# One decoder step on one core: the first attention operands loaded during the decode, and the fourth w_up split moved from GpSimd to VectorE

## The chip, the cores and the metric

The kernel runs on one core of a Trainium2 chip. The metric is the time of one execution on the device in microseconds (us). The core has five engines that work side by side, each through its own queue of instructions in order: TensorE (PE, matrix products; PEld is its loading of weights), VectorE (DVE), ScalarE (ACT), GpSimd (POOL) and SyncE (SP, which here only issues DMAs). GpSimd issues DMAs too. An instruction that waits for a semaphore holds up everything behind it on its engine.

## The reference: what is computed

One layer of a decoder over two inputs: a prompt of 1024 tokens and 8 samples of 4 new tokens each with 1024 cached positions. Model width is 1024.

```python
h = rms_norm(x, n1) * (1 + sc1) + sh1
q_a, k_a, v_a, q_b, f_b, i_b, g_b = split(h @ w_in)
q_a, k_a = rms_norm(q_a, qg), rms_norm(k_a, kg)
o_a = stick_breaking(q_a, k_all, v_all, positions, sb_b)      # 8 heads of 64
o_b = hgrn2(...)                                              # gated recurrence, 8 heads of 64
x = x + g1 * (concat(o_a, o_b) @ w_out)
h2 = rms_norm(x, n2) * (1 + sc2) + sh2
x = x + g2 * (square(relu(h2 @ w_up)) @ w_down)               # w_up 1024 x 4096
```

For the prompt, keys and values are those of the prompt itself. For the samples, `k_all` and `v_all` are read from a paged cache through a page table (64 pages of K, 64 of V, 128 positions each) with the new tokens behind them; that part is called the decode here. In stick-breaking attention the weight of a key is sigmoid(z) times the product of 1 - sigmoid(z') over the keys between it and the query, which the kernel takes with a reversed cumulative product (a scan) over each row.

## The kernel before, in words

Products are made in float32r with both operands split into a high and a low part: hi is a cast of x (ScalarE, line 151), lo is x - hi (line 152). Each product is then three matmuls: hi by hi, lo by hi, hi by lo. A piece of a weight is 128 x 1024: `weight` (line 154) loads it into wraw (2 buffers), casts it into whi and subtracts into wlo (5 buffers each), at a raised priority. The argument `e` names the engine of the subtraction, VectorE where nothing is given.

The work goes in stages: projections, recurrence with the attention of the first 512 prompt tokens, output projection of those tokens, then from about 550 to 1100 us the stage of this change, then the output projection of the other 512 and the sample tokens, and their MLP up to the end. q and k of the prompt are written to DRAM (`qkd`, high and low parts) early on, and read back head by head.

In the stage of the change two chains of work are interleaved on the engines (line 1470). One is the first MLP (`mlp`, line 1183), which runs 8 blocks of 512 columns of w_up; in a block four pieces of w_up (m = 0 to 3), then four pieces of w_down. `GL = (3,)` gives the subtraction of the fourth piece to GpSimd. The other chain is `decode_and_attention` (line 1439): first the decode of the samples (`decode`, line 563), its later part beside the recurrence of the samples (`hgrn_decode`, line 962), then the attention of the second 512 prompt tokens (`attention`, line 879) over 8 heads.

For each head the attention loads qh and ql (line 891, both halves of the partitions hold the same 64 rows) and kk (line 892, high and low part of k) and vhl (line 894). All are issued by GpSimd, two buffers each, from a pool that is opened once the decode's pools are closed. Then for each 128 queries: z = two products (lines 905, 906), sigmoids on ScalarE (909, 910), masks on GpSimd (913, 914), the scan on VectorE (919), a product on GpSimd (920), transposes on PE (932), the split into wh and wl (151, 152), and the products with V (941, 942).

The recurrence of the samples loads its states s0b (line 972) by GpSimd as well, two for each step and half, each once the half before is used.

The order of instructions on an engine is not written out by hand. The tile framework plans it before the run, from the order of emission, raised priorities and a timeline of its own (`schedule_with_timeline_sim=True`, line 1507).

The first MLP's pool (`rp`, line 1465) holds one g2b tile of 128 x 1024 and two xres tiles of 128 x 512. In before these are written in the last block of the MLP only.

Of the kernel before, what the change touches and what calls it, by code (L numbers as in the profile page):

```python
# [9 lines left out]
F32 = mybir.dt.float32  # L10
F32R = mybir.dt.float32r
# [9 lines left out]
P = 128  # L21
D = 1024
KT = 8
T = 1024
# [9 lines left out]
NBE0, NBE, NHB, NWA, NU, NRW, NX2, NF = 4,8,3,4,4,4,3,3  # L34
ORDER = (4,5,8,6,7)
NWH, NOM, SPL, NRAW, NRC, NAT = 2,3,7,4,2,1
PV, PQ, PW, PH = [162, 417, 315, 427]
GL, GD = (3,),()
BO = dict(o="0167", r="45")
KS0 = "wwwwwuup"  # L40
KS1 = "5p 0w 6p 1w 7p 2w 3u 4u"
# [40 lines left out]
def hymba_step(ctx, tc, x_p, x_s, ck, cv, st_in, ptab, c_p, c_s, w_ada, b_ada, n1g, n2g, w_in,  # L82
# [3 lines left out]
    V, S, G, TE = nc.vector, nc.scalar, nc.gpsimd, nc.tensor  # L86
# [14 lines left out]
    def pool(name, side="left", stack=ctx, **kw):  # L101
        return stack.enter_context(tc.tile_pool(name=name, bufs=1, side=side, reuse_waits="tile", **kw))
# [7 lines left out]
    qkd = dp.tile([2, 2, 4, P, T], F32, name="qkd")  # L110
# [449 lines left out]
                                nc.sync.dma_start(qkd[what, part, 2 * p2:2 * p2 + 2, :, rows].rearrange("a p t -> p a t"),  # L560
                                                  tt.rearrange("p a u t -> p a (u t)").bitcast(F32))

    def decode(pd_):

        qbd = pd_.tile([P, 2, 544], F32, name="qbd", tag="qbd", bufs=1)
        G.memset(qbd, 0.0)
# [38 lines left out]
        ms = pd_.tile([P, 4, NB, 4], F32, name="ms")  # L605
# [35 lines left out]
        for gz in range(2):  # L641
            be = bes[gz]

            qbf = pd_.tile([P, 4, 32], F32, name="qbf")
            G.memset(qbf, 0.0)
            for p in range(4):
                for hh in range(2):
                    rr, o = slice(64 * hh, 64 * hh + 64), 4 * hh
# [15 lines left out]
            for k0 in (0, 4, 8):  # L664
                n, r = (4, P) if k0 < 8 else (1, NS)
# [9 lines left out]
            for b4 in range(4):  # L675
                b = 4 * gz + b4
# [18 lines left out]
                for hh in range(2):  # L695
                    r = slice(64 * hh, 64 * hh + 64)
# [179 lines left out]
        with tc.high_priority(offset=PH):  # L876
            norm()

    def attention(pb, ms, nbe):

        q0, nq, nk = 256 * ms[0], 256 * len(ms), 256 * (ms[-1] + 1)
        both = lambda t, part, p, r, cs: qkd[t, part, p, r, cs].unsqueeze(0).to_broadcast([2, 64, cs.stop - cs.start])
        for p in range(4):
            for hh in range(2):
                h = 2 * p + hh
                hr = slice(64 * hh, 64 * hh + 64)

                qh, ql = (pb.tile([P, nq], F32R, name=name, bufs=2) for name in ("qh", "ql"))
                kk_ = pb.tile([P, nk], F32R, name="kk", bufs=2)
                for part, tile_ in enumerate((qh, ql)):  # L890
                    G.dma_start(tile_, both(0, part, p, hr, slice(q0, q0 + nq)))
                G.dma_start(kk_, qkd[1, :, p, hr, 0:nk])
                vhl = pb.tile([P, nk // P, P], F32R, name="vhl", bufs=2)
                G.dma_start(vhl, vd[0:nk, P * h:P * (h + 1)].rearrange("(t p) x -> p t x", p=P))
                for m in ms:
                    ws = []
                    for i in (2 * m, 2 * m + 1):
                        n = (i + 1) * P
# [26 lines left out]
                    for kb in range(0, 2 * m + 2, 2):  # L925
# [12 lines left out]
                        for a in range(2):  # L938
                            cs = slice(P, 256) if diag and a == 1 else slice(0, 256)
# [22 lines left out]
    def hgrn_decode(p1):  # L962
# [63 lines left out]
        for j in range(4):  # L1026
# [10 lines left out]
             lambda n, p=ga: p.tile([P, 2048], F32, name="wada", bufs=NAR)[:, 0:512 * n], "ada")  # L1037
# [4 lines left out]
    qstack.close()  # L1042
    gh = hgrn(pool("hgrn", stack=gstack))
    gb = attention(pool("attn0", stack=astack), (0, 1), NBE0)

    def until(g, x):
# [136 lines left out]
    def mlp(h_hi, h_lo, chunks, fp, nx, side=iter(())):  # L1183
# [1 line left out]
        r_hi = [h_hi[:, k] for k in range(KT)]  # L1185
        r_lo = [h_lo[:, k] for k in range(KT)]
        n = chunks[-1].stop
        g2b = fp.tile([P, D], F32, name="g2b")
        acc = [lp.tile([P, HW], F32, name=f"acc{c}", tag="acc", bufs=8) for c in range(KT)]
        for blk in range(NBLK):  # L1190
            u_hi, u_lo, ws = [], [], []
# [20 lines left out]
            if blk == 0:  # L1212
                for cs in parts:
                    for m in range(NK):
                        up(m, cs)
                    yield
            if blk == NBLK - 1:
                nc.sync.dma_start(g2b, g2d.to_broadcast([P, D]))
            for half_ in range(2):

# [218 lines left out]
    def decode_and_attention():  # L1439
        banks.update(BD)  # L1440
        with ExitStack() as es:
            gd = decode(pool("decode", stack=es))
            for _ in range(33):
                next(gd)
                yield
            banks.update(BV)
            yield from side_by_side((gd, 28), (hgrn_decode(pool("hgrn_s", stack=es)), W[4]))
        banks.update(BA)
        with ExitStack() as es:
            yield from attention(pool("attn1", stack=es), (2, 3), NBE)  # L1450

    def h2_tiles():
        return hp2.tile([P, KT, HW], F32R, name="h2_hi", tag="h2_hi", bufs=1), hp2.tile([P, KT, HW], F32R, name="h2_lo", tag="h2_lo", bufs=1)
# [11 lines left out]
    rp = pool("res", side="right", stack=rstack)  # L1465
# [45 lines left out]
```

## Time and profile before

| | us |
|---|---|
| median of 3 runs | 1550.24 |
| lowest, highest run | 1548.09, 1552.9 |
| profiled execution | 1546.85 |
| its span, first to last instruction | 1545.1 |
| TensorE busy in the span | 1489.3 (96%) |
| VectorE busy | 1083.4 (70%) |
| ScalarE busy | 642.7 (42%) |
| GpSimd busy | 345.4 (22%) |

All views below are of the profiled execution, with times in us from the start of its span. A busy time is the sum over an engine's instructions; "idle before" with an arrow says how long the engine stood still before an instruction and what ended the wait. The granted clock is a share of TensorE's full clock of 2.4 GHz.

### The profile page before, as it was taken

The page shows a single profiled execution, that of the slowest core. Times are in us where ns is not written, and L with a number is a line of the kernel's source. Part 1 is how long each engine was busy: PE and PEld are TensorE (multiplying, and loading weights), DVE is VectorE, ACT ScalarE, POOL GpSimd, SP SyncE. Part 2 cuts the span into 40 slices and gives each one's busy share as a digit, 9 for nine tenths or more (in the row PEclk, how much of TensorE's full clock was granted, in tenths as well). Part 3 has the DMA queues.
Part 4 walks back from the last instruction along what each step waited for, and adds up shares of the span by engine and source line. Part 5 has one row for each costly group of instructions (what it writes and reads, how often), then busy time and mean ns, then how long its engine had stood idle before and what let it go on. Part 6 is the DMA issues. An engine that isn't in the chain of part 4 may idle for free. (4 is left out here: it accounts for less than half of the span.)

```text
span 1545.1 us, 26232 instructions
## 1 busy us (share of the span) xinstructions
PE 1489.3 (96%) x9521; PEld 1257.0 (81%) x9521; DVE 1083.4 (70%) x2288; ACT 642.7 (42%) x1219; POOL 345.4 (22%) x560
## 2 busy tenths in 40 slices
PE   7999999999999989999997999999999999999998
PEld 3666689999999787775665788888578999999998
DVE  4976438888876783455554888888688567777775
ACT  3742234443422454333232666664245533343340
POOL 0200125634210030000121676694200000000000
PEclk8999999999999999999998999999999999999999
DMA  9389873423123456668677366552654333323222
GB/s 325 118 278 309 265 231 68 106 58 92 37 77 114 140 172 219 218 216 256 199 160 121 88 133 121 119 113 74 237 164 125 105 96 96 92 84 99 84 82 86
DMA packets 249414, 223.14 MB, mean 144 GB/s; under 512 B 60507, under 2 KB 196259, under 8 KB 247236
## 3 DMA queue, kind: packets, MB, share of 16 engines
q1 hardware_dynamic: 186308, 199.26, 41.0%
q0 software_dynamic: 62976, 22.20, 8.8%
q8 instruction: 75, 1.23, 0.3%
q14 instruction: 55, 0.45, 0.1%
HBM read 190.14 MB, written 31.11 MB: 143 GB/s over the span
## 5 line engine op out<-in xcount | busy, mean ns | idle before, releaser
L204 PE MATMUL pm<-h_hi,whi 128*128 128x384 f32 (+3 forms) x800 | 273.0, 343 | 6.0 <-DVE h_hi L335 3.0
L205 PE MATMUL pm<-h_lo,whi 128*128 128x384 f32 (+3 forms) x800 | 272.2, 341 | 0.3
L206 PE MATMUL pm<-h_hi,wlo 128*128 128x384 f32 (+3 forms) x800 | 271.7, 340 | 0.0
L151 ACT CAST whi<-wraw 128x1024 fp32r<-128x1024 f32 x136 | 142.8, 1053 | 217.8 <-PE pm L205 128.0
L152 DVE TENSOR_TENSOR wlo<-wraw,whi 128x1024 fp32r<-128x1024 f32 x128 | 169.1, 1321 | 89.6 <-ACT whi L151 83.6
L204 PEld LDWEIGHTS pm<-h_hi,whi 128*128 128x128 f32 x800 | 151.5, 190 | 24.3 <-issue 6.4
L206 PEld LDWEIGHTS pm<-h_hi,wlo 128*128 128x128 f32 x800 | 152.1, 190 | 10.6 <-issue 2.0
L205 PEld LDWEIGHTS pm<-h_lo,whi 128*128 128x128 f32 x800 | 152.2, 190 | 10.2 <-DVE h_lo L336 0.8
L206 PE MATMUL pm<-uh,wlo 128*128 128x272 f32 x512 | 145.2, 289 | 0.0
L205 PE MATMUL pm<-ul,whi 128*128 128x272 f32 x512 | 144.8, 288 | 0.0
L204 PE MATMUL pm<-uh,whi 128*128 128x272 f32 x512 | 139.8, 289 | 0.4 <-ACT uh L1327 0.4
L919 DVE TENSOR_TENSOR_SCAN om<-om 128x128 f32<-128x128 f32 (+3 forms) x96 | 112.3, 1174 | 25.4 <-POOL om L913 20.3
L1228 PE MATMUL pm<-whi,uh 128*128 128x512 f32 x256 | 104.7, 409 | 3.3 <-DVE acc L1236 3.3
L920 POOL TENSOR_TENSOR be<-be,om 128x384 f32<-128x384 f32 (+3 forms) x96 | 100.5, 1056 | 23.9 <-DVE om L919 20.0
L1229 PE MATMUL pm<-wlo,uh 128*128 128x512 f32 x256 | 101.9, 399 | 0.0
L1230 PE MATMUL pm<-whi,ul 128*128 128x512 f32 x256 | 101.7, 402 | 0.0
L205 PEld LDWEIGHTS pm<-ul,whi 128*128 128x128 f32 x512 | 95.9, 188 | 0.2 <-DVE ul L1328 0.2
L206 PEld LDWEIGHTS pm<-uh,wlo 128*128 128x128 f32 x512 | 95.9, 188 | 0.1
L204 PEld LDWEIGHTS pm<-uh,whi 128*128 128x128 f32 x512 | 93.4, 188 | 0.7 <-ACT uh L1327 0.7
L217 PE MATMUL pm_qkv<-whi,h_lo 128*128 128x512 f32 x192 | 77.3, 403 | 1.1 <-DVE h_lo L336 0.8
L215 PE MATMUL pm_qkv<-whi,h_hi 128*128 128x512 f32 x192 | 77.2, 403 | 0.4 <-DVE rs_i L138 0.3
L216 PE MATMUL pm_qkv<-wlo,h_hi 128*128 128x512 f32 x192 | 76.4, 398 | 0.0
(404 smaller groups left out, 3408.5 us busy)
## 6 DMA issues: line engine op xcount, KB each, us to landing
wraw<-in_w_down_dram SPq DMA_DIRECT2D x64, 512.0 KB, 5.7
wraw<-in_w_up_dram SPq DMA_DIRECT2D x40, 512.0 KB, 5.6
wada<-in_w_ada_dram SPq DMA_DIRECT2D x16, 1024.0 KB, 8.7
raw<-in_cache_k_dram SPq DMA_DIRECT2D x64, 256.0 KB, 3.2
vt<-in_cache_v_dram SPq DMA_DIRECT2D x64, 256.0 KB, 4.6
wraw<-in_w_in_dram SPq DMA_DIRECT2D x24, 512.0 KB, 5.9
uraw<-in_w_up_dram SPq DMA_DIRECT2D x24, 512.0 KB, 3.8
wa<-in_w_ada_dram SPq DMA_DIRECT2D x16, 512.0 KB, 6.4
```

The costliest lines, as they stand in the source:

```text
L151: (V.tensor_copy if h is V else S.copy)(hi, src)
L152: (e or V).tensor_tensor(lo, src, hi.bitcast(F32), op=sub)
L204: TE.matmul(pm, w_hi[:, k, :], r_hi[k][:, cs], start=(k == ks[0]), stop=False)
L205: TE.matmul(pm, w_hi[:, k, :], r_lo[k][:, cs], start=False, stop=False)
L206: TE.matmul(pm, w_lo[:, k, :], r_hi[k][:, cs], start=False, stop=(k == ks[-1]))
L215: TE.matmul(pm, h_hi[:, k, cs], hi, start=(k == 0), stop=False)
L217: TE.matmul(pm, h_lo[:, k, cs], hi, start=False, stop=(k == KT - 1))
L919: V.tensor_tensor_scan(back, back, back, 1.0 if right is None else right[:, 0:1], op0=mult, op1=ALU.bypass)
L920: G.tensor_tensor(be[:, 0:w], be[:, 0:w], om[:, 1:w + 1], op=mult)
L1228: TE.matmul(pm, u_hi[m][:, ts], hi, start=(m == 0), stop=False)
L1229: TE.matmul(pm, u_hi[m][:, ts], lo, start=False, stop=False)
L1230: TE.matmul(pm, u_lo[m][:, ts], hi, start=False, stop=(m == NK - 1))
```

## The change

Four edits in one:

1. `GL` is empty, so the fourth piece of w_up in each block of the first MLP is split on VectorE, as the other three are.
2. The three loads qh, ql and kk are made a function `load_qk`. For head 0 of the second attention it is called inside `decode`, behind the memset of qbf of the second group of samples, and told to be issued after that memset.
3. The tiles of these three loads are taken from the first MLP's pool: qh0 and ql0 in the two buffers of xres, kk0 in the buffer of g2b. The first attention is as before.
4. The tile g2b of the first MLP is taken in the last block, in the same buffer.

vhl of head 0, and all loads of the other heads, stay where they are.

```diff
-GL, GD = (3,),()
+GL, GD = (),()
...
-    def decode(pd_):
+    def decode(pd_, first):
...
-            G.memset(qbf, 0.0)
+            mark = G.memset(qbf, 0.0)
+            if gz == 1:
+                with tc.issue_after(mark.ins):
+                    load_qk(*first, 0, 512, 512, T)
...
+    def load_qk(qh, ql, kk, h, q0, nq, nk):
+
+        hr = slice(64 * (h % 2), 64 * (h % 2) + 64)
+        for part, x in enumerate((qh, ql)):
+            G.dma_start(x, qkd[0, part, h // 2, hr, q0:q0 + nq].unsqueeze(0).to_broadcast([2, 64, nq]))
+        G.dma_start(kk, qkd[1, :, h // 2, hr, 0:nk])
...
-                qh, ql = (pb.tile([P, nq], F32R, name=name, bufs=2) for name in ("qh", "ql"))
-                kk_ = pb.tile([P, nk], F32R, name="kk", bufs=2)
-                for part, tile_ in enumerate((qh, ql)):
-                    G.dma_start(tile_, both(0, part, p, hr, slice(q0, q0 + nq)))
-                G.dma_start(kk_, qkd[1, :, p, hr, 0:nk])
+                if h == 0 and first:
+                    qh, ql, kk_ = first
+                else:
+                    qh, ql = (pb.tile([P, nq], F32R, name=name, bufs=2) for name in ("qh", "ql"))
+                    kk_ = pb.tile([P, nk], F32R, name="kk", bufs=2)
+                    load_qk(qh, ql, kk_, h, q0, nq, nk)
...
-        g2b = fp.tile([P, D], F32, name="g2b")
...
             if blk == NBLK - 1:
+                g2b = fp.tile([P, D], F32, name="g2b", tag="g2b")
                 nc.sync.dma_start(g2b, g2d.to_broadcast([P, D]))
...
-            gd = decode(pool("decode", stack=es))
+            first = [rp.tile([P, n], F32R, name=name, tag=tag, bufs=b)
+                     for name, n, tag, b in (("qh0", 512, "xres", 2), ("ql0", 512, "xres", 2), ("kk0", T, "g2b", 1))]
+            gd = decode(pool("decode", stack=es), first)
...
-            yield from attention(pool("attn1", stack=es), (2, 3), NBE)
+            yield from attention(pool("attn1", stack=es), (2, 3), NBE, first)
```

## Rows read from the trace of the kernel before

**Rows 1.** The page, part 1: busy us (share of the span) and instructions of each engine.

```profile
PE 1489.3 (96%) x9521; PEld 1257.0 (81%) x9521; DVE 1083.4 (70%) x2288; ACT 642.7 (42%) x1219; POOL 345.4 (22%) x560
```

**Rows 2.** Who waited for whom, whole span, PE: us in total, times, longest.

```profile
PE pz L905 <- DMA kk<-qkd: 11.7, 1, 11.7
PE ptx L318 <- DVE xr L1172: 3.8, 1, 3.8
```

**Rows 3.** Windows of 10 us: PE, PEld, DVE, ACT, POOL busy, granted clock, DMA.

```profile
810.00:820.00 10.00, 0.56 (x3) 0.12 (x1) 1.82 (x2) 0.24 (x1) 0.00 (x0) 0.77 1.88 144
820.00:830.00 10.00, 7.78 (x29) 6.34 (x29) 3.93 (x4) 2.85 (x6) 3.89 (x5) 0.72 0.81 154
```

**Rows 4.** PE in order of time around 820: start, us, line, out<-in, idle before.

```profile
809.93 0.40 PE L1229 MATMUL pm<-wlo,uh 128*128 128x512 f32 x1
810.16 0.40 PE L1230 MATMUL pm<-whi,ul 128*128 128x512 f32 x1
822.22 0.45 PE L905 MATMUL pz<-kk,qh 128*128 128x128 f32 x1 [11.65 <-DMA kk<-qkd]
...
825.02 0.63 PE L1228 MATMUL pm<-whi,uh 128*128 128x512 f32 x1
825.45 0.48 PE L1229 MATMUL pm<-wlo,uh 128*128 128x512 f32 x1
```

**Rows 5.** ACT in order of time, first instruction behind the gap.

```profile
822.89 1.05 ACT L151 CAST whi<-wraw 128x1024 fp32r<-128x1024 f32 x1 [12.65 <-PE pz L906]
```

**Rows 6.** POOL in order of time: the second qbf memset, the last state loads, kk.

```profile
664.27 0.20 POOL L645 MEMSET qbf<- 128x128 f32 x1 [46.37 <-PE pzn L653]
671.23 0.10 POOL L656 MEMSET dom<- 128x1 f32 x1 [6.75 <-DVE dbe L660]
...
795.63 1.23 POOL L972 DMA_DIRECT2D s0b<-in_state_hgrn_dram  x2 [4.88 <-DVE sw L1008]
...
798.48 0.83 POOL L892 DMA_DIRECT2D kk<-qkd  x1
```

**Rows 7.** DMA issues of 795 to 830: count, KB each, median us to landing.

```profile
kk<-qkd POOLq DMA_DIRECT2D x2, 512.0 KB, 25.5
vhl<-vd POOLq DMA_DIRECT2D x2, 512.0 KB, 27.9
...
qh<-qkd POOLq DMA_DIRECT2D x2, 256.0 KB, 18.4
```

**Rows 8.** PE and POOL in order of time: first product with V, first g2b use.

```profile
869.27 0.28 PE L941 MATMUL pv<-wh,vhl 128*128 128x256 f32 x1
...
1015.18 2.54 POOL L1241 TENSOR_TENSOR acc<-acc,g2b 128x512 f32<-128x512 f32 x2
```

**Rows 9.** Line 152 by operation: duration ns min/median/max, first and last start.

```profile
L152 DVE TENSOR_TENSOR wlo<-wraw,whi x128: 1193/1225/3355, 86.8 to 1494.9; 128x1024 fp32r<-128x1024 f32 x128
...
L152 POOL TENSOR_TENSOR wlo<-wraw,whi x8: 2372/2442/2786, 544.6 to 1042.4; 128x1024 fp32r<-128x1024 f32 x8
```

**Rows 10.** DVE in order of time: first and last of seven splits beside POOL's.

```profile
546.01 2.23 DVE L152 TENSOR_TENSOR wlo<-wraw,whi 128x1024 fp32r<-128x1024 f32 x1 [0.50 <-ACT whi L151]
...
1042.94 3.35 DVE L152 TENSOR_TENSOR wlo<-wraw,whi 128x1024 fp32r<-128x1024 f32 x1
```

**Rows 11.** Window of the attention, columns as in rows 3.

```profile
860.00:1062.00 202.00, 194.04 (x1037) 164.05 (x1036) 173.05 (x200) 128.22 (x241) 156.81 (x218) 1.00 0.55 114
```

**Rows 12.** Who waited for whom, 855 to 1062.

```profile
DVE wlo L152 <- ACT whi L151: 7.4, 10, 2.9
...
PE pv L942 <- DVE wl L152: 3.6, 3, 1.3
PE pm L1228 <- DVE acc L1236: 3.3, 3, 1.3
```

**Rows 13.** A window of the decode (columns as in rows 3), and landing of V pages.

```profile
660.00:680.00 20.00, 20.00 (x127) 15.25 (x125) 13.20 (x16) 9.28 (x18) 0.30 (x2) 1.00 0.67 202
...
DMA to landing us min/median/max: 3.6/4.6/5.5
```

More of the change, by code (lines that the diff above doesn't have):

```diff
@@ L877, in hgrn, with attention @@
             norm()
-    def attention(pb, ms, nbe):
+    def load_qk(qh, ql, kk, h, q0, nq, nk):
[3 more added lines that the diff above has]
+        G.dma_start(kk, qkd[1, :, h // 2, hr, 0:nk])
+    def attention(pb, ms, nbe, first=None):
         q0, nq, nk = 256 * ms[0], 256 * len(ms), 256 * (ms[-1] + 1)
-        both = lambda t, part, p, r, cs: qkd[t, part, p, r, cs].unsqueeze(0).to_broadcast([2, 64, cs.stop - cs.start])
         for p in range(4):
```

## The prediction, made before the changed kernel ran

> **What bounds the kernel now.** I read the page first. TensorE (PE) is busy 1489.3 of 1545.1 us [rows 1], so at most 55.8 us can be had without removing matmuls, and only from places where PE stands still. The list of who waited for whom, PE's rows alone, has one long entry: the product of q and k at line 905 waited 11.7 us, once, for the transfer into kk; the next longest is 3.8 us [rows 2]. Two windows of 10 us show where: PE has 0.56 us of work in 810 to 820 and 7.78 in 820 to 830, and the granted clock stands at 0.77 and 0.72 there [rows 3]. PE's own order of time gives the edges: the last matmul of the MLP starts at 810.16, the first of the second attention at 822.22, after 11.65 us of idle. Matmuls of one shape start 0.23 us apart before the gap and still 0.43 us apart at 825.02 [rows 4].
>
> Is kk the only thing late there? In 810 to 820 VectorE works 1.82 us, ScalarE 0.24 and GpSimd not at all [rows 3], and ScalarE's wait of 12.65 us ends with the second of those two products [rows 5]. Nothing but the transfer holds the kernel. Its cause is on GpSimd's queue [rows 6]: the loads of the recurrent state sit ahead, each waiting for VectorE, the last at 795.63; right behind come qh and ql, at 798.48 kk, then vhl of head 0 and the same four of head 1. The two loads of kk took a median 25.5 us to land, those of vhl 27.9 [rows 7].
>
> **Part one, the early loads.** Moved: qh, ql and kk of head 0, three DMAs, from behind the state loads to behind the second memset of qbf, at 664.27 [rows 6]. Nothing is added in bytes. On GpSimd's queue they take some 2.5 us of issue (three by the 0.83 of kk in rows 6) and the next item there starts at 671.23; GpSimd is idle in between, so the issue costs nothing. No semaphore is added ahead of other work that the queue would do: the state loads come next after 671 and wait for VectorE anyway. The new tiles lie in buffers of the first MLP's pool that are not written before its last block, whose first use of g2b starts at 1015.18; head 0, whose first product with V is at 869.27 [rows 8], is through with kk over 100 us earlier (eight heads take the 240 us from 822 to 1062), so the sharing costs nothing either. On SP no DMA changes place except the g2b load, which now has that old release to wait for.
>
> How soon do they land? Bounds: no row shows such a load in the decode. The nearest are the same loads in the crowd of 797 to 825, 18.4 us for qh to 25.5 for kk [rows 7]. At the worst of these they are there by about 693, 117 us before PE wants them. The margin carries the argument, not the value.
>
> What PE gets back: the idle 11.65 us, and the slow matmuls. With the granted clock at 1.00 or half of it (2.4 and 1.2 GHz), means of 0.77 and 0.72 are 4.6 and 5.6 us at the low level, 10.2 in all. It fell after matmuls had ceased at 810 and, the second window beginning low, rose at about 820 + 5.6 = 825.6, which the wide spacing at 825.02 bears out [rows 3, 4]. Of the 10.2 us, the part after 822.2 is 3.4, and at half speed half of that is lost: 1.7 us. Sum: 13.35 us.
>
> Does something else stop PE at 810? What head 0 wants next is vhl, for the first product with V at 869.27, 47 us after the first product with k [rows 8]. In the changed kernel it heads the crowd on GpSimd's queue, lands by about 797 + 28 = 825 even if it takes as long as now, and is wanted at about 856. The transfers left behind the state loads (vhl of head 0, all of head 1) are 1 MB lighter. In the attention behind it PE is busy 194.04 of 202 us [rows 11], so no second wait of that size follows. I take the whole 13.35 and keep 8 as a lower end, for pages below.
>
> **Part two, the fourth w_up piece.** One of four pieces in each of eight blocks moves its low part (line 152) from GpSimd to VectorE. GpSimd loses 8 instructions of 2442 ns median; VectorE gains 8 of 1225 ns, 9.8 us [rows 9]. But the two get in each other's way: in seven of the eight cases VectorE's own split ran beside GpSimd's and took 2.23, 1.62, 2.42, 2.07, 2.38, 2.72 and 3.35 us, from the one at 546.01 to the one at 1042.94 [rows 10]. That is 16.8 us where seven by 1.225 would be 8.6: 8.2 us lost, which the change gives back. Net, VectorE gets 1.6 us more over 500 us. From 838 on, where VectorE matters, four splits add 4.9 us and remove 10.5 - 4.9 = 5.6. I count this part at zero on PE. The cover for it is VectorE's slack: it is busy 173.05 of 202 us in 860 to 1062 [rows 11], and PE's waits for VectorE there sum to only about 7 us, 3.6 and 3.3 [rows 12]. Ends of the range: -5 us (these waits mostly vanish) to +9.8 (all on PE's path).
>
> **Sum.** The profiled execution took 1546.85 us, 1.75 beyond its span, and 1546.85 - 13.35 = 1533.5. The median of the three runs shown, 1550.24, stands 3.4 above that execution; carried over, the forecast is 1536.9, say 1537. A measurement of this kernel tells about 0.3% (4.7 us) from no change.
>
> **Rivals.** *Pages late.* The early loads share the DMA engines with the decode's cache pages and the weights, which already move 202 GB/s in 660 to 680 [rows 13]. One MB at 202 GB/s is 5.2 us. If the pages are pushed back by that and PE, which multiplies them in order, waits for all of it, 13.35 shrinks to 8.2: 1542. Against it: PE is full in that window, so it waits for no page there; a page of V lands in 4.6 us, at most 5.5 [rows 13]. The Trainium skill (DMA: Bandwidth & Descriptors, section Issuing engines are not separate DMA queues) says that transfers run on the same 16 engines and interleave whichever engine issued them, which is the rule that speaks for this rival; the crowd of rows 7 agrees with it.
>
> *VectorE saturated.* If the moved splits cost their full 9.8 us on PE's path, the gain is 3.5: 1546.7, no change that shows. For it: 86% busy in the attention. Against: the blocked splits of rows 10, which come back. The Trainium skill (Perfetto Trace Analysis, section Optimizing Scalar/DVE Operations) says that work may be taken off a saturated VectorE to GpSimd, and this change does the reverse; the same section grants that the two share a read port, and rows 10 show what that costs here.
>
> *The gap stays.* The instructions' order on each engine comes from a planner's own timeline, so the three loads might be placed behind the state loads again, or PE might meet another late operand at 810. The time is then 1550, unchanged. Against: the early loads' only stated predecessor is the memset, and all other engines stood idle in the gap [rows 3].
>
> *Slower: VectorE held.* A split waits for ScalarE's cast of the same piece. GpSimd could wait without harm. On VectorE, the scans, the additions that free PE's banks and the low parts of w stand behind it in order. The price for each, if PE stands for all of it, is at most the longest such wait in the attention: 2.9 us in ten [rows 12]. Eight are 23.2 us, and 1550.24 - 13.35 + 23.2 = 1560. It decides from 13.35 / 8 = 1.7 us of PE idle per moved split; the mean of the ten waits is 0.74, and much of that is hidden, so it is unlikely.
>
> **How the numbers follow.** The forecast gets 0.66, with a range of its own from 1531 to 1542; late pages 0.09, VectorE saturated 0.09, the gap staying 0.08, VectorE held 0.08. From 1530 (5 us of small waits gone besides the gap, and 2 more for scatter) to 1548 the first three cases are held, 0.84; the two left out have 0.16. Faster by over 0.3% means below 1545.6: the first two cases and a third of the third, 0.78. Within 0.3%: the rest of the third and the gap staying, 0.14. Slower: 0.08.
>
> **What would show it.** Right: no wait of line 905 for kk above 1 us, a granted clock of 1.00 across the change from decode to attention, the three loads on GpSimd's queue near 665, and PE's idle time lower by about 12 us. In part two no GpSimd split at line 152, VectorE's at 136 with none near 3 us for that reason, and PE's waits for VectorE in the attention still below about 10 us. Wrong: PE waiting for raw or vt in 665 to 700 (late pages); those waits for VectorE at 15 us or more (saturated or held, told apart by whether VectorE is busy or waits for casts); or a new gap of several us at the first products of the attention with another releaser.

## The result and the profile after: 18 us slower, not 13 faster

| | before | after |
|---|---|---|
| median, us | 1550.42 (4 runs) | 1568.82 (4 runs) |
| lowest, highest | 1548.09, 1552.90 | 1565.46, 1570.30 |
| span of the profiled execution | 1545.1 | 1567.9 |

The ratio of after to before is 1.0115, with a 95% interval from 1.0092 to 1.0139. The forecast was 1537.0 and the range ended at 1548. The two profiled executions lie 22.8 us apart and the medians 18.4, so some 4 us of what is read from the profiles below is scatter between executions.

Lines of the second attention and what follows are 11 higher after the change (906 is 917). The page, part 1, of after:

```profile
PE 1501.1 (96%) x9521; PEld 1264.4 (81%) x9521; DVE 1078.8 (69%) x2296; ACT 641.0 (41%) x1219; POOL 320.6 (20%) x552
```

Against [rows 1], the span grew by 22.8 us. TensorE's busy time grew by 11.8 with the same 9521 instructions, so the same matmuls ran longer; its idle time grew from 55.8 to 66.8, by 11.0. Lost time is thus of two kinds, standing still and running at the low clock after it.

The names in the lines that follow: pz is a product of q and k, pv a product with V, wl the low part of the attention's weights, ptd the transposes of raw pages of K, pm a product of the MLP. pm_os and pm_o are the output projection of the samples and of the prompt, and woraw is a raw piece of its weight w_out. Who waited for whom, PE of after (total, times, longest):

```profile
PE pv L953 <- DVE wl L152: 8.2, 3, 5.6
PE pm_os L1119 <- DMA woraw<-in_w_out_dram: 6.9, 2, 5.3
PE ptd L633 <- DMA raw<-in_cache_k_dram: 5.7, 3, 2.4
...
PE pm L1239 <- ACT rr L1208: 3.2, 1, 3.2
PE pz L916 <- ACT be L921: 2.4, 1, 2.4
```

The 11.7 us for kk [rows 2] is gone. Five entries have grown in its place (the wait for wl was 3.8 us in before), most of them in three stretches; one more, 3.5 us for tp, lies in the output projection behind. Windows of after (columns as in rows 3):

```profile
680.00:700.00 20.00, 16.95 (x83) 11.98 (x84) 5.36 (x10) 2.99 (x5) 0.00 (x0) 0.91 0.63 187
810.00:820.00 10.00, 8.52 (x44) 5.99 (x43) 3.50 (x8) 0.82 (x2) 5.56 (x11) 1.00 1.62 217
820.00:830.00 10.00, 9.39 (x51) 7.36 (x51) 5.96 (x8) 2.61 (x4) 1.66 (x4) 1.00 1.44 169
1100.00:1120.00 20.00, 8.91 (x43) 6.02 (x41) 8.50 (x13) 2.64 (x5) 5.08 (x4) 0.67 0.47 150
1120.00:1140.00 20.00, 17.88 (x71) 10.41 (x72) 8.78 (x11) 8.57 (x10) 0.00 (x0) 0.82 0.82 257
```

and of before, where no row of them stands above:

```profile
680.00:700.00 20.00, 20.00 (x105) 12.01 (x103) 5.83 (x15) 4.34 (x6) 2.38 (x1) 1.00 0.67 234
1100.00:1120.00 20.00, 16.63 (x72) 8.48 (x70) 15.91 (x16) 8.06 (x10) 5.22 (x3) 1.00 0.86 297
1120.00:1140.00 20.00, 19.69 (x89) 15.29 (x86) 16.00 (x41) 9.61 (x19) 0.00 (x0) 1.00 0.75 227
```

At 810 to 830 PE now works 17.9 of 20 us at a clock of 1.00 where it worked 8.3 [rows 3]. That is what was forecast. But it has lost 3 us in 680 to 700, and 7.7 us in 1100 to 1120, with the clock down to 0.67 after the standstill.

**First place: pages of K.** PE of after in order of time (start, duration, what, idle before), first the old gap's place, then the decode, then the stage's end:

```profile
807.13 0.22 PE L916 MATMUL pz<-kk,qh 128*128 128x128 f32 x1
```

```profile
677.78 0.63 PE L633 MATMUL ptd<-ident,raw 128*128 128x128 f32 x4 [1.97 <-DMA raw<-in_cache_k_dram]
680.69 0.63 PE L633 MATMUL ptd<-ident,raw 128*128 128x128 f32 x4 [1.34 <-DMA raw<-in_cache_k_dram]
683.68 1.08 PE L633 MATMUL ptd<-ident,raw 128*128 128x128 f32 x4 [2.36 <-DMA raw<-in_cache_k_dram]
```

```profile
1110.55 0.58 PE L953 MATMUL pv<-wl,vhl 128*128 128x256 f32 x1 [5.60 <-DVE wl L152]
1117.79 1.07 PE L1119 MATMUL pm_os<-woraw,smp_k 128*32 128x512 f32 x2 [5.30 <-DMA woraw<-in_w_out_dram]
```

The first product of the attention waits for nothing. In the decode, transposes of raw K pages wait three times. The DMA issues of 664 to 690 (KB each, median us to landing), after and then before:

```profile
raw<-in_cache_k_dram SPq DMA_DIRECT2D x8, 256.0 KB, 9.1
...
kk<-qkd POOLq DMA_DIRECT2D x1, 512.0 KB, 21.8
...
qh<-qkd POOLq DMA_DIRECT2D x1, 256.0 KB, 10.8
ql<-qkd POOLq DMA_DIRECT2D x1, 256.0 KB, 14.9
```

```profile
raw<-in_cache_k_dram SPq DMA_DIRECT2D x7, 256.0 KB, 2.6
```

The early loads go out at 666.46 to 668.09, where they were put. Of the pages in each window the trace gives the landing of a single one: 9.1 us after the change (the page issued at 678.44), 2.6 in before (the one of 670.02). PE multiplies the pages in order, so one late page holds all behind it.

**Second place: late pieces of w_up.** The stretch 979 to 1000 of after, engine by engine: SP, ScalarE, VectorE, PE (start, duration, idle before).

```profile
979.74 6.80 SPq L161 DMA_DIRECT2D wraw<-in_w_up_dram  x2
988.27 5.76 SPq L957 DMA_DIRECT2D mixa<-tv  x1
```

```profile
988.61 0.65 ACT L1210 CAST uh<-rr 128x512 fp32r<-128x512 f32 x1
997.68 1.04 ACT L151 CAST whi<-wraw 128x1024 fp32r<-128x1024 f32 x1 [8.42 <-DMA wraw<-in_w_up_dram]
```

```profile
998.76 1.23 DVE L152 TENSOR_TENSOR wlo<-wraw,whi 128x1024 fp32r<-128x1024 f32 x1 [7.76 <-ACT whi L151]
```

```profile
999.85 0.50 PE L1239 MATMUL pm<-whi,uh 128*128 128x512 f32 x1 [3.16 <-ACT rr L1208]
```

ScalarE's cast of a piece waits 8.42 us for its transfer, VectorE's split behind it 7.76, and everything queued behind them on both engines stands, until PE has nothing left. In [rows 12] the longest such wait of VectorE is 2.9. What ends PE's wait is ScalarE's rr, queued behind the cast, and not the split, which is still running at 999.85. The piece is the first of the last block, issued at 979.74: its split was on VectorE in before too. The fourth piece of that block comes late in the same way:

```profile
1037.61 1.04 ACT L151 CAST whi<-wraw 128x1024 fp32r<-128x1024 f32 x1 [7.66 <-DMA wraw<-in_w_up_dram]
```

PE's 2.4 us for be, at 1039.87, stand behind it. The two pieces went out 1.5 and 1.1 us behind the kk of a later head (978.24 and 1018.10), and 17.9 and 18.4 us pass from their issue to their cast. The late piece of `loads_only` below is alike: 0.3 us behind a kk, and 19.0 us to its cast. That the kk is what delays them was not tried apart.

**Third place: the end of the stage.** VectorE of after there, and SP of before and of after (start, duration, idle before):

```profile
1100.97 1.76 DVE L1256 TENSOR_TENSOR xres<-xres,yy 128x512 f32<-128x512 f32 x1 [3.47 <-POOL xres L1253]
...
1109.20 0.69 DVE L1256 TENSOR_TENSOR xres<-xres,yy 128x512 f32<-128x512 f32 x1 [3.75 <-POOL xres L1253]
1109.81 1.02 DVE L152 TENSOR_TENSOR wl<-ptw,wh 128x512 fp32r<-128x512 f32 x2
```

```profile
1095.11 0.85 SPq L1122 DMA_DIRECT2D woraw<-in_w_out_dram  x2
```

```profile
1113.36 0.47 SPq L957 DMA_DIRECT2D mixa<-tv  x1
1113.89 0.58 SPq L1133 DMA_DIRECT2D woraw<-in_w_out_dram  x1
```

The last head's split wl stands on VectorE behind two additions of the MLP's last block. These wait for GpSimd, and GpSimd waits for the loads of xres (the residual, from x1d), for which there are two buffers. PE waits 5.60 us for that wl. The last head's store to mixa (the attention's result, which the projection reads) comes late for the same reason, and on SP the first loads of w_out stand behind it: 1113.89 where before had 1095.11. PE waits 5.30 us more. The wait for xres is not new. VectorE of before has it as well, at a time when PE still has matmuls of the MLP to do, up to 1099.1:

```profile
1099.65 0.69 DVE L1245 TENSOR_TENSOR xres<-xres,yy 128x512 f32<-128x512 f32 x1 [5.03 <-POOL xres L1242]
```

Why is the last head at the very end? The planner's orders differ. In before, 48 matmuls of the first MLP follow the last product with V (line 942), so that the head's end, its stores and the first w_out loads are covered by them. After the change none does: 16 products with V follow the MLP's last matmul, and all eight residual additions stand ahead of the last wl on VectorE.

Milestones of some kernels of the next section are in one table. The columns are starts in us: of GpSimd's memset of qbd (with which the decode starts there), of the decode's last product with V, of the MLP's last matmul, of the attention's last product with V, and of the last pm_o product of the output projection.

| kernel | decode starts | decode ends | MLP ends | attention ends | projection ends |
|---|---|---|---|---|---|
| before | 564.7 | 783.2 | 1099.1 | 1088.0 | 1158.9 |
| after | 566.7 | 792.9 | 1103.1 | 1112.0 | 1181.8 |
| split edit alone (`gl_only`) | 566.1 | 786.1 | 1099.7 | 1107.7 | 1174.6 |
| early loads alone (`loads_only`) | 570.4 | 796.9 | 1103.9 | 1092.8 | 1166.8 |
| early loads alone, moved (`move01`) | 566.9 | 785.1 | 1093.2 | 1082.1 | 1154.3 |
| after, early loads moved (`move_gl`) | 563.8 | 782.1 | 1091.9 | 1101.9 | 1171.9 |
| after, both tail edits (`tail_both`) | 563.7 | 789.5 | 1101.0 | 1102.0 | 1170.8 |

Of the 22.9 us to the projection's end 9.7 are there when the decode ends (2.0 of them at its start), 3.2 come up to the stage's last matmul though the gap of 13.35 is gone from there, and 10.0 behind it.

What the split edit does shows best against the early loads alone. The decode takes 226 us in both kernels (218 to 219 in before and with the early loads moved). From its end to the MLP's end it is 310 us with the split edit and 307 without. Then 8.9 us pass to the attention's end, which without the edit lies ahead of the MLP's. From the later of these two ends to the projection's it is 70 us against 63. The sum is 3 + 9 + 7 = 19 us, nearly all of it behind the MLP's last matmul.

### The profile page after: what moved, and what is told of

It reads as the page before. It is cut to its first block, busy times and chain, and to the rows that moved or that the text cites. A ratio compares the mean times of both kernels' runs of the same rounds, so it can differ in the third digit from the quotient of the medians.

```text
span 1567.9 us, 26233 instructions
## 1 busy us (share of the span) xinstructions
PE 1501.1 (96%) x9521; PEld 1264.4 (81%) x9521; DVE 1078.8 (69%) x2296; ACT 641.0 (41%) x1219; POOL 320.6 (20%) x552
## 3 DMA queue, kind: packets, MB, share of 16 engines
q0 software_dynamic: 62976, 22.20, 8.6%
## 4 chain that ended last, share of the span: by engine, by line
PE 75%; DVE 10%; DMA 8%; issue 3%; ACT 2%; POOL 1%; SPq 0%; DVEq 0%; ACTq 0%; POOLq 0%
PE pm L204 11%; PE pm L205 11%; PE pm L206 11%; PE pm_qkv L217 3%; PE pm L1239 3%; PE pm_qkv L215 3%; PE pm_u L1323 3%; PE pm_u L1325 3%; PE pm_qkv L216 3%; PE pm_u L1324 3%; PE pm L1241 3%; PE pm L1240 3%; DMA wraw<-in_w_up_dram 3%; PE ptd L633 2%; DVE wlo L152 1%
## 5 line engine op out<-in xcount | busy, mean ns | idle before, releaser
L152 DVE TENSOR_TENSOR wlo<-wraw,whi 128x1024 fp32r<-128x1024 f32 x136 | 172.4, 1269 | 95.8 <-ACT whi L151 95.2
L206 PEld LDWEIGHTS pm<-h_hi,wlo 128*128 128x128 f32 x800 | 152.7, 191 | 11.4 <-issue 2.8
L930 DVE TENSOR_TENSOR_SCAN om<-om 128x384 f32<-128x384 f32 (+3 forms) x96 | 105.9, 1107 | 23.5 <-POOL om L924 17.1
L931 POOL TENSOR_TENSOR be<-be,om 128x128 f32<-128x128 f32 (+3 forms) x96 | 99.4, 1045 | 31.1 <-DVE om L930 23.0
```

The lines of the kernel that those rows point to most:

```text
L152: (e or V).tensor_tensor(lo, src, hi.bitcast(F32), op=sub)
L206: TE.matmul(pm, w_lo[:, k, :], r_hi[k][:, cs], start=False, stop=(k == ks[-1]))
L930: V.tensor_tensor_scan(back, back, back, 1.0 if right is None else right[:, 0:1], op0=mult, op1=ALU.bypass)
```

## The experiments

Times are medians; the ratio is to before, run in four groups, each with its runs of before on the same chip (four rows of the table, four, four, three; before: 1550.43, 1550.59, 1549.58 and 1549.67).

| run | us | lowest, highest | ratio [95%] |
|---|---|---|---|
| gl_only | 1561.94 | 1560.99, 1568.13 | 1.0082 [1.0054, 1.0110] |
| loads_only | 1549.34 | 1541.30, 1553.30 | 0.9986 [0.9971, 1.0001] |
| after_nocast | 1569.07 | 1564.00, 1570.85 | 1.0113 [1.0088, 1.0139] |
| before_nocast | 1548.94 | 1546.17, 1551.27 | 0.9994 [0.9984, 1.0004] |
| hold | 1554.49 | 1551.95, 1556.54 | 1.0030 [1.0017, 1.0043] |
| hold_move | 1545.48 | 1542.34, 1550.46 | 0.9973 [0.9960, 0.9985] |
| after_w174 | 1581.40 | 1579.48, 1584.14 | 1.0208 [1.0191, 1.0225] |
| pool_first4 | 1551.56 | 1541.50, 1554.42 | 1.0002 [0.9984, 1.0019] |
| hold_mid | 1545.64 | 1541.81, 1550.81 | 0.9977 [0.9961, 0.9993] |
| move01 | 1538.16 | 1531.33, 1548.17 | 0.9924 [0.9885, 0.9964] |
| after_g_blk47 | 1562.02 | 1560.98, 1564.12 | 1.0081 [1.0054, 1.0107] |
| hold_mid_p4 | 1541.33 | 1538.14, 1547.62 | 0.9953 [0.9935, 0.9970] |
| tail_store | 1569.79 | 1567.71, 1574.66 | 1.0125 [1.0103, 1.0148] |
| tail_both | 1559.49 | 1558.31, 1562.57 | 1.0069 [1.0047, 1.0091] |
| move_gl | 1561.57 | 1558.39, 1563.71 | 1.0076 [1.0052, 1.0100] |

### The two halves apart

`gl_only` is before with the split edit, `loads_only` is after without it.

```diff
 gl_only, on before:      -GL, GD = (3,),()   +GL, GD = (),()
 loads_only, on after:    -GL, GD = (),()     +GL, GD = (3,),()
```

> Only edit 1 of the change: the fourth w_up piece split on VectorE, the loads as before. Theory A (the loss behind 980 us comes from edit 1, through the order that the planner lays anew up to the end of the attention): about 1550 + 18 to 25 = 1568 to 1575 us, with the gap before the first products of the second attention still there (about 11 us) and a stall of several us behind the MLP's last matmul. Theory B (the early loads cause all of it, edit 1 is neutral): 1548 to 1553 us.

> Edits 2 to 4 without edit 1: the early loads, with the fourth w_up piece split on GpSimd as before. Theory A: the gap goes (13 us), the K pages' wait and the low clock behind it cost some 8, so 1550 - 5 = 1545 us, within 3, and no stall behind the MLP's last matmul. Theory B: the whole loss is here, 1566 to 1570 us, with the stall of 5 us or more for the w_out loads near 1115.

The split edit alone costs 11.5 us (1561.94 - 1550.43). Beside the early loads it costs 19.5 (1568.82 - 1549.34). The early loads alone are worth 1.1 us and not 13.35, an interval that ends at no change. Theory A had the place of both losses, but both times missed its ranges, by 6 and by 1 us. PE's waits in the first:

```profile
PE pz L905 <- DMA kk<-qkd: 12.7, 1, 12.7
PE pv L942 <- DVE wl L152: 5.8, 5, 4.4
PE pm_os L1108 <- DMA woraw<-in_w_out_dram: 5.3, 1, 5.3
```

The old gap stands, as it must, and the two waits of the stage's end are there without the early loads. Its order at the end is that of after (16 products with V behind the MLP); the order of `loads_only` there is that of before (48 MLP matmuls behind). So the end belongs to the split edit, and the order, not the loads, goes with it. By the milestones the MLP of `gl_only` ends 0.6 us after that of before: what it loses, it loses behind that.

In `loads_only` the gap is gone, the pages of K are late (4.3 us on PE), and one wait is new. PE, then ScalarE, then SP:

```profile
833.60 1.11 PE L1017 MATMUL pds<-ve,kts 32*64 32x256 f32 x4 [4.84 <-ACT kts L1009]
```

```profile
832.34 1.04 ACT L151 CAST whi<-wraw 128x1024 fp32r<-128x1024 f32 x1 [7.03 <-DMA wraw<-in_w_up_dram]
```

```profile
813.34 0.39 SPq L161 DMA_DIRECT2D wraw<-in_w_up_dram  x1
```

A w_up piece issued at 813.34 is used at 832.34. Around it GpSimd issues vhl of head 0, all of head 1 and then, at 814.72 to 816.27, q and k of head 2: the attention's own buffers of head 0 were never taken, so head 2's loads move up into them.

### Is it the packets?

The loads of q and k go from float32 in DRAM into tiles of float32r, and their queue moves 352 bytes a packet on average (22.20 MB in 62976 packets). Both kernels with these loads written through a float32 view of the tile, in the same order of instructions:

```diff
-            G.dma_start(x, qkd[0, part, h // 2, hr, q0:q0 + nq]....)
-        G.dma_start(kk, qkd[1, :, h // 2, hr, 0:nk])
+            G.dma_start(x.bitcast(F32), qkd[0, part, h // 2, hr, q0:q0 + nq]....)
+        G.dma_start(kk.bitcast(F32), qkd[1, :, h // 2, hr, 0:nk])
```

> The changed kernel with the loads of qh, ql and kk (all heads, both attentions) written through a float32 view of their tiles, so that source and destination have one type; bytes, queue and the order of instructions on every engine stay those of the changed kernel. If the many small packets of these loads (352 bytes on average on that queue) are what delays the K pages and later the w_up pieces: under 1000 packets fewer bytes apart for the early loads, no wait for raw above 1 us, ScalarE's waits for w_up under 40 us in sum, and about 1550 us. If the order itself is at fault: at least 1562 us, the stall behind the MLP unchanged.

> The kernel before with the same float32 view for the loads of qh, ql and kk; order of instructions as before. If packets made kk late: it lands in under 15 us instead of 25, the wait of 11.65 us shrinks to 0 to 4 us, and the time falls by 8 to 13 us to 1537 to 1542. If the transfer is late for its bytes or for vhl's packets beside it: the gap stays above 8 us and the time within 0.3% of 1550.

The page, part 3, for GpSimd's queue, after and then `after_nocast`:

```profile
q0 software_dynamic: 62976, 22.20, 8.6%
```

```profile
q0 software_dynamic: 42496, 22.20, 7.5%
```

A third of the packets is gone, in the window of the early loads too (2096 for 3120). PE's wait for pages falls from 5.7 to 4.2, the gap of before from 11.7 to 10.1, and neither time moves by more than its interval. So this third of the packets is not the cause. What far fewer packets would do is not shown.

### Where the early loads' gain went

`hold` is `loads_only` with head 2's loads of q and k held until head 0's last product on GpSimd. `hold_move` also moves the early loads from 666 to behind the state loads of the second recurrence step (kk at 731.63).

```diff
+                    with ExitStack() as es:
+                        if h == 2 and first:
+                            es.enter_context(tc.issue_after(mark.ins))
                         load_qk(qh, ql, kk_, h, q0, nq, nk)
...
                     load_state(j + 1, g)
+                    if (j, g) == (0, 1):
+                        with tc.issue_after(mark.ins):
+                            load_qk(*first, 0, 512, 512, T)
```

> The early loads with the fourth w_up piece on GpSimd (as in loads_only), and head 2's q and k loads held on GpSimd's queue behind head 0's last product, so that 2 MB and not 3 MB land together behind the state loads. Theory A2 (in loads_only the crowd kept its size, because head 2's loads came forward into the free buffers, and the w_up piece issued at 813 landed some 19 us later): ScalarE's wait of 7.0 us for that piece falls under 3 us, PE's 4.8 us behind it to under 2 us; 3 to 6 us less than loads_only, 1543 to 1546. Rival (other traffic delays the piece): the wait stays and the time is within 2 us of loads_only.

> As hold, and head 0's early loads stand behind the state loads of the second step (about 735 us) instead of the qbf memset, when all K pages have landed. Theory A2: the waits for K pages (4.3 us, with the low clock about 6) go as well and no wait for V pages takes their place: 1537 to 1541 us, faster than both kernels. Rival (V pages are hit instead): PE waits of 2 us or more for vt, and the time is that of hold.

The first missed, at 5.2 us above `loads_only` (1554.49 - 1549.34): the wait for kts fell to 1.1 us, but head 2's own kk, now issued at 875.32, made PE wait in its place:

```profile
PE pz L919 <- DMA kk<-qkd: 5.1, 1, 5.1
```

The second has that same wait (5.0) and none for pages, and is 9.0 us below the first (1554.49 - 1545.48): the late pages cost that. It too missed its range, which ended at 1541. `hold_mid` releases head 2 some 15 us sooner than `hold_move` (kk at 852.79, not 868.11), behind the first pair of row blocks (`if h == 0 and m == ms[0]: mark = prod`); `move01` moves the early loads and holds nothing.

> Theory A (the early loads' own gain is the gap of 13.35 us; what took it back is only where transfers meet, first beside the K pages, then beside the w_up piece and at head 2's own start): with the early loads behind the state loads of the second step, and head 2's loads released after head 0's first pair of row blocks (about 855 us) instead of its last product (866 us), no wait of TensorE for raw pages, the wait for kts under 1.5 us and the wait for kk under 1.5 us, 1538 to 1543 us. Rival B (any place for head 2's 1 MB of loads costs some 5 us, because the work behind it merely waits elsewhere): 1544 to 1548 us, with a wait of 4 to 6 us of TensorE somewhere in 850 to 900.

> The early loads behind the second step's state loads, head 2's loads not held. Theory A: no wait for raw pages, the wait for kts behind the late w_up piece stays at 4 to 5 us, no wait for head 2's kk; 1542 to 1547 us, the same as with head 2 held to head 0's last product. Rival B (the wait for kts costs nothing, it only moves idle time forward): 1538 to 1541 us.

In `hold_mid` neither wait is left (PE waits nowhere for kk or kts), yet its median is that of `hold_move`, in rival B's range and without the wait that rival B named. `move01` keeps a wait of 5.4 us for kts and has the lowest median of all, again in rival B's range. Their profiled spans are 1540.1 and 1540.0, and the runs of `move01` reach from 1531 to 1548. So theory A's ranking failed, the two can't be told apart, and the wait for kts is not shown to cost anything.

What is shown is that edits 2 to 4 alone gain with the loads behind the second step: 5.1, 3.9 and 11.4 us in `hold_move`, `hold_mid` and `move01` (1550.59 - 1545.48, 1549.58 - 1545.64, 1549.58 - 1538.16; the last by its interval 5.6 to 17.8). In the milestones of `move01` the stage from the decode's start to the MLP's end is 8.1 us shorter than in before (526.3 against 534.4). The forecast 13.35 lies in the interval of this one run and is not confirmed.

### What the split edit does: load on VectorE, or order?

First the weight by which the planner interleaves decode and attention with the MLP, to pull the last head forward again:

```diff
-W = [66, 24, 9, 166, 4]
+W = [66, 24, 9, 174, 4]
```

> The changed kernel with one weight of the interleaving altered, so that decode and attention are emitted a little earlier beside the MLP (166 to 174). All w_up pieces stay on VectorE. By its order of instructions 24 matmuls of the MLP stand behind the last product with V on PE, where the changed kernel has none (and 16 products with V behind the MLP's last matmul), and the kernel before has 48. Theory A (edit 1 costs through the order at the end of the stage): the waits of 5.6 and 5.3 us near 1110 fall under 2 us each, 1569 falls to 1552 to 1558. Rival (VectorE's extra splits in the attention cost by themselves): 1563 us or more.

It failed by 23 us. 24 MLP matmuls follow the last product with V again, and at the end PE waits 4.0 us for woraw and no longer for wl. But the weight also rules the decode:

```profile
680.00:800.00 120.00, 112.86 (x521) 60.06 (x519) 51.30 (x101) 25.84 (x39) 4.97 (x8) 0.96 0.69 207
```

PE issues 521 matmuls there, and 620 in after. The time lies in the rival's range, but the run tells nothing on the end alone. The pair that does changes only which blocks keep a split on GpSimd, half of them in each:

```diff
-                ws.append(piece([wview(...)], KT, P, G if m in GL else V))
+                ws.append(piece([wview(...)], KT, P, G if m == 3 and blk < 4 else V))    pool_first4
+                ws.append(piece([wview(...)], KT, P, G if m == 3 and blk >= 4 else V))   after_g_blk47
```

> The changed kernel with the fourth w_up piece of the first four blocks (those beside the decode) back on GpSimd; the four beside the attention stay on VectorE. Its order has 24 MLP matmuls behind the last product with V too. Theory A: like after_w174, 1552 to 1558 us, though every split of the attention's stretch is still on VectorE. Rival (VectorE's load in the attention): 1563 us or more, as only splits where VectorE has slack were moved.

> The change with the fourth pieces of blocks 4 to 7 split on GpSimd and those of blocks 0 to 3 on VectorE, the mirror of the run with blocks 0 to 3 on GpSimd, so as many splits on each engine. Theory A (the planned order at the stage's end decides): in this kernel's order the last products of pv stand behind all but one of the MLP's matmuls and 6 of 8 residual additions before the last split of weights, much as in the change, so 1557 to 1568 us, with a wait of pv for wl or of pm_os for woraw of 4 us and more after 1095 us. Rival B (VectorE's load decides, and half of the splits given back to GpSimd is enough): 1549 to 1554 us, as the mirror.

`pool_first4` has every split beside the attention on VectorE, as after has, with 24 MLP matmuls behind the last product with V; it takes 1551.56, 2.2 us above `loads_only`, and the two intervals overlap. `after_g_blk47` gives those splits back to GpSimd, so VectorE has less to do where it is busiest; but the programs end with the last product with V behind the MLP, and it takes 1562.02, with one long wait at the end:

```profile
1113.44 1.07 PE L1119 MATMUL pm_os<-woraw,smp_k 128*32 128x512 f32 x2 [11.85 <-DMA woraw<-in_w_out_dram]
```

That is the opposite of what VectorE's load would give, and what the order gives. `hold_mid_p4` repeats `pool_first4` with the loads moved and head 2 held as in `hold_mid`:

> As the run with head 2 released after head 0's first pair and the early loads moved, but with the fourth pieces of blocks 4 to 7 on VectorE and those of blocks 0 to 3 on GpSimd. Theory A (splits on VectorE cost nothing where the planned order at the end stays): within 4 us of that run, 1538 to 1547 us. Rival B (VectorE's load beside the attention costs by itself): 6 to 10 us longer than that run.

1541.33: half of the splits on VectorE cost nothing there either. A cover of 24 matmuls is not a whole one: PE still waits for woraw, 4.0 us in `pool_first4` and 4.6 in `hold_mid_p4`.

### What the end itself costs

Two repairs of the end, on after, with the split edit kept. `tail_store` puts the last head's stores to mixa on GpSimd's queue; `tail_both` also gives the last residual addition to GpSimd, so that no instruction of VectorE waits for xres.

```diff
-                    nc.sync.dma_start(mixa[m][64 * h:64 * h + 64, :], tv)
+                    (G if h == 7 else nc.sync).dma_start(mixa[m][64 * h:64 * h + 64, :], tv)
...
-                            V.tensor_tensor(xr, xr, yy, op=add)
+                            G.tensor_tensor(xr, xr, yy, op=add)
```

> The change with the last head's stores to mixa on GpSimd's queue instead of SyncE's; the orders of TensorE and VectorE at the stage's end stay (16 products of pv behind the MLP's last matmul, all residual additions before the last split of weights). Theory A (the first loads of w_out stand behind the last store on SyncE): they go out some 4 us earlier, behind the output stores instead of the last store of mixa, the wait of pm_os for woraw falls from 5.3 to under 2 us, 1562 to 1567 us. Rival B (the wait for woraw only hides another one behind it): 1567 to 1571 us.

> As the run with the last stores on GpSimd's queue, and the last of the two additions to xres on GpSimd too, so that no instruction of VectorE waits for the x1d loads. Theory A (the two waits at the stage's end are most of what the split edit costs beyond the early loads): the wait of pv for wl at the end falls from 5.6 to under 1.5 us, that for woraw too, 1553 to 1560 us. Rival B (the time is lost over the whole stage, 960 to 1060 us as well, and the end only shows it): 1561 to 1568 us.

The first gives nothing, as rival B had it: the w_out loads then go out behind the output stores, at 1117.48, and PE's waits for woraw fall only from 6.9 to 5.3 us. The second gains 9.3 us on after (1568.82 - 1559.49), near the upper end of theory A. The wait for wl falls from 5.6 to 1.2 us, and by the milestones the stage ends 10.0 us sooner, of which 3.4 were there when the decode ended. The wait for woraw stays:

```profile
1108.20 1.07 PE L1119 MATMUL pm_os<-woraw,smp_k 128*32 128x512 f32 x2 [5.92 <-DMA woraw<-in_w_out_dram]
```

and so do the waits near 998 and 1038 us, 2.9 and 2.7. So VectorE's waits for xres at the end are some third to a half of the 19.5 us (6.6 by the milestones, 9.3 by the times): the 8.9 us from the MLP's end to the attention's are 1.0 here, the 70 us of the projection 69. No run takes the late w_out loads away in this order, so their share, the 7 us of the projection, is read from the milestones and not tried.

Last, the whole change with its early loads moved as in `move01`:

> The change whole, its early loads moved behind the state loads of the second decode step. Theory A (the pages' lateness costs 5.7 us of waiting and some 2 us of the clock, and the end of the stage is apart from it): no wait of TensorE for raw pages, the waits at the end as in the change, 1558 to 1564 us. Rival B (with the splits all on VectorE the decode's earlier end is lost again in the attention): 1566 to 1571 us.

1561.57, as theory A had it: 7.3 us below after, no wait for pages. Its end is that of after, in PE's waits:

```profile
PE pv L950 <- DVE wl L152: 9.4, 3, 6.8
PE pm_os L1120 <- DMA woraw<-in_w_out_dram: 6.3, 2, 5.2
```

Against `move01` this prices the split edit at 23.4 us (1561.57 - 1538.16), with the range of `move01` on it; by the milestones it is 20.6.

## Why the prediction was wrong

**The gap** went as worked out: no wait for kk, a clock of 1.00 across it, three loads on GpSimd's queue at 666. The step "I take the whole 13.35" failed as a sum, because of what the loads do elsewhere: `loads_only` gains 1.1 us. As a size it is in reach of `move01` (11.4 us by the times, 8.1 by the milestones), no more. And the bound of 55.8 us, from which the text starts, takes PE's busy time as fixed; it moved by 11.8.

**"The issue costs nothing" and "the margin carries the argument".** These costed the early loads by GpSimd's time and by their own due time. What they left out is the other transfers of that window: the pages of K had no margin there. The rival *late pages* had the mechanism and a price (5.2 us) close to what was measured: 5.7 us of waiting, and 7.3 us by `move_gl`, 9.0 by `hold_move`, with the low clock after each wait (0.91 in 680 to 700). It was given 0.09 because "PE is full in that window, so it waits for no page there" [rows 13]. That is no evidence: a full PE shows that pages come in time, not by how much. The row to read was how soon a page is used after it lands. The rule that was set beside it (the Trainium skill, DMA: Bandwidth & Descriptors, section Issuing engines are not separate DMA queues) was the better guide; this trace agrees, as far as one timed page in each window goes, 2.6 us to 9.1.

**"The transfers left behind the state loads are 1 MB lighter"** failed: head 2's loads took the freed buffers and moved into the same crowd, as `loads_only` shows. It made a new wait of 4.8 us, which could not be shown to cost time. The borrowed buffers, too, are "not written before its last block" in the order of the program alone. In time, SP of before fills them early: the loads of xres start at 564.83 and 578.09, that of g2b at 578.47. After the change all three go out at 865.84 to 866.72, so three DMAs changed place on SP and not one. No wait of PE names them.

**"I count this part at zero on PE. The cover for it is VectorE's slack"** is the step that cost most, 11.5 to 23 us, beyond the upper end of 9.8 that it was given. Read as a change of load, it was right: no split of line 152 is left on GpSimd, VectorE has 136 and its busy time fell by 4.6 us, and in `pool_first4` the splits beside the attention cost nothing that shows. VectorE is not saturated either: it works 162.8 of 207 us in 855 to 1062. What it left out is that the instruction's engine is an input of the planner, which lays a different order down to the stage's end. The text says itself that the order comes "from a planner's own timeline", but under *the gap stays*, and for three loads alone.

***Slower: VectorE held*** had the sign, and with 1560 the nearest time, but that is luck as far as the trace goes. VectorE's idle time before these splits did rise, its longest from 2.9 to 7.8 us. But both times what was late was a transfer ahead of ScalarE's cast, PE's wait ended with ScalarE, and the piece of 999.85 was not one of the moved ones. Its price went by the number of moved splits, and the pair of runs with equal numbers on either side differ by 10.5 us (1562.02 - 1551.56).

The decisive thing was not in any rival: the cover of 48 MLP matmuls at the stage's end. The row that could have warned is SP's load of woraw at 1095.11, ahead of the MLP's last matmul at 1099.1. By the milestones, losing that cover goes with the 9 and the 7 us.

What stays open: why the planner's order turns when the splits of blocks 0 to 3 change engine and not when those of 4 to 7 do, whether the kk beside them is what makes the two pieces of w_up late, and why a load of kk takes some 20 us to land. The order was never changed alone, with every split on the same engine as in after and the decode left as it is; that it is the cause rests on the pair of runs, on `tail_both` and on the milestones. Both tail repairs together with the moved loads weren't tried.

## What to carry to other kernels

Where a planner orders the instructions, moving even a cheap one to another engine is a change of the whole order: compare the two programs at the ends of the stages (what follows the last product of each chain, what stands ahead of the next stage's first load) before pricing the instruction. A transfer moved forward is priced at the transfers it lands among: look for the consumer with the least time between landing and use, and for what moves up into the place it leaves. Here the early loads behind the second recurrence step, without the split edit, were the fastest version found, 1538.16 us (ratio 0.9924, from 0.9885 to 0.9964; its six runs reach from 1531 to 1548).

## What the runs showed of the hardware

A standstill cost more than its length here. After the waits of 5.60 and 5.30 us the sample's products ran at the low of the two clock levels (1.2 GHz, granted clock 0.67 in 1100 to 1120). PE of after, duration in ns, lowest, median, highest:

```profile
L1119 PE MATMUL pm_os<-wraw,smp_q x12: 592/1060/1063, 1117.9 to 1131.8; 128*32 128x512 f32 x12
```

In before the median of the same twelve is 592. And a load far from the crowd was hardly quicker: kk landed 21.8 us after its issue amid the decode, beside qh, ql, the pages and two pieces of weights, and 25.5 in the crowd of [rows 7]. The kk of the later heads, one head at a time, took 17.8 to 20.0 us (of after).
